# A two-layer hybrid trunk on one core: all engines in written order, evictions one block of weights apart, v from blocks of 256 rows, rotations between the conv blocks

## The chip, the core and the metric

The kernel runs on one core of a Trainium2 chip. The time is device microseconds; the median of 3 runs of the kernel before is 892.13 us (891.50 to 892.79). Five engines work side by side, each through its own list of instructions: TensorE (PE; its weight loads are shown as PEld), VectorE (DVE), ScalarE (ACT), GpSimd (POOL) and SyncE (SP, which here only starts DMAs). TensorE's granted clock is 1.2 or 2.4 GHz; the profile writes it as a share of full speed.

## The reference

```python
def hybrid_layer(x, ...):
    h = rmsnorm(x, norm_mix)
    cb, cc, cu, q, k, v, g, ga, gb = split(h @ w_in)
    y_conv = (cb * causal_conv3(cc * cu)) @ w_conv_out
    o = retention(rotary(q), rotary(k), v)           # 4 heads, decayed causal scores
    o = (o - mean(o)) * rsqrt(var(o) + EPS) * ret_norm
    y_ret = (silu(g) * o) @ w_ret_out
    x = x + (sigmoid(ga) * y_conv + sigmoid(gb) * y_ret) @ w_o
    h2 = rmsnorm(x, norm_mlp)
    return x + square(relu(h2 @ w_up)) @ w_down
# two layers, then a final rmsnorm; 256 tokens, width 1024, d_ff 4096, float32
```

## The kernel before

All weights are cut on the host into 152 blocks of 1 MB (128 partitions x 2048 float32), 76 a layer: 32 of w_in (1024 contraction rows x 256 columns each), 4 each of w_conv_out (`yc`), w_ret_out (`yr`) and w_o (`mg`), 16 of w_up and 16 of w_down. They pass in one fixed order, and every block goes through the same stations. SP starts its DMA into a `raw` buffer. ACT rounds it to a high part (`split`, L99), in two halves of 128 x 1024, and DVE subtracts (L100) to get the low part; both stand in a `parts` buffer. PE then does 16 pairs of products (`proj`, L171 and L172): high weights against high and low activations (512 columns), low weights against high activations (256 columns). The result, in a PSUM tile `ps`, is evicted by `collect` (L209 on ACT, L210 on DVE), and what follows (rotation, gate, conv) is done on DVE, ACT and POOL.

There are 3 `raw` buffers, 3 `parts` buffers and 3 `ps` tiles. Blocks are split up to AHEAD = 2 ahead (`next_block`). Small work that belongs to later blocks is put off by a number of blocks (`later`). The program is recorded in this order, but `schedule_with_timeline_sim=True` lets a scheduler, by its own simulated times, choose the order in which each engine's instructions stand.

The w_in blocks of a layer come as v (4), four triples cc, cu, cb of the conv branch, q (2), k (2), g (4), ga (4), gb (4). In layer 0 the first v block is multiplied in plain float32 without being split (`whole_tokens`, L130 to L140), while its data arrives in five pieces, each with a piece of `px` (x and the gains), all on SP. Six products on zeros (`warm`, L319) come ahead. A v block gives one head of v for all tokens; `value` (L407 to L416) reduces it on DVE (L409), subtracts the mean on POOL (L412), and splits it. The sums over all channels that a norm needs are two small products with ones (`mix_st`, `mlp_st`, and `var_ps` for the heads; L231 and L232).

Of the kernel before, what the change touches and what calls it, by code (L numbers as in the profile page):

```python
# [28 lines left out]
FIRST = ((1, 1, 2, 2, 2), (2, 2, 4), (4, 4))  # L29
AHEAD = 2  # L30
WARM = 6


Q0, K0, V0, G0, GA0, GB0 = 3072, 3584, 4096, 5120, 6144, 7168
IN_ORDER = (
    [("v", V0 + 256 * i) for i in range(4)]
    + [(n, o + 256 * i) for i in range(4) for n, o in (("cc", 1024), ("cu", 2048), ("cb", 0))]
    + [("q", Q0), ("q", Q0 + 256), ("k", K0), ("k", K0 + 256)]
    + [("g", G0 + 256 * i) for i in range(4)]
# [3 lines left out]
BLOCKS_PER_LAYER = 32 + 4 * 3 + 16 + 16  # L43
# [5 lines left out]
def trunk_kernel(ctx, tc, px, pos, w, cst, mask, out):  # L49
# [4 lines left out]
    raw_p = ctx.enter_context(tc.tile_pool(name="raw", bufs=3))  # L54
# [17 lines left out]
    idle = tmp.tile([P, 2 * T], BF16, tag="tmp", bufs=5, name="idle")  # L72
# [8 lines left out]
    class Parts:  # L81


        def __init__(self, name):
            self.tiles = [s8.tile([P, KT // 2, 2, T], F32R, tag="s8", name=f"{name}{i}") for i in range(2)]
# [9 lines left out]
    def t2(name, tag="tmp", bufs=5):  # L95
        return tmp.tile([P, 2, T], F32, tag=tag, bufs=bufs, name=name)
# [14 lines left out]
    def load_block(i):  # L111
        raw, parts = block_tiles()
        nc.sync.dma_start(out=raw.rearrange("p a b -> p (a b)"), in_=w[i])
        for p in range(2):
            split_block(raw, parts, slice(p * KT, (p + 1) * KT))
        return parts

    cnt = [0]

    ready = {}  # L120

    def next_block():
        i = cnt[0]
        cnt[0] += 1
        for j in range(i, min(i + AHEAD + 1, w.shape[0])):
            if j not in ready:
                ready[j] = load_block(j)
        return ready.pop(i)

    def whole_tokens(xs):  # L130

        ps = ps_main.tile([P, 2, 2, T], F32, tag="mm", name="ps")
        raw = next_block()
        for k in range(KT):
            for j in range(2):
                mm(ps[:, j, 0], xs[:, k, j * P:(j + 1) * P], raw[:, 2 * k:2 * k + 2, :], k == 0, k == KT - 1)
        run_waiting()
        t = t2("sum", "sum", 4)
        nc.scalar.copy(t, ps[:, :, 0, :])
        return t  # L140


    waiting = []

    def later(n, fn, *args):
        waiting.append([cnt[0] + n, fn, args])

    def run_waiting(everything=False):
        while True:
            due = [e for e in waiting if everything or e[0] <= cnt[0]]  # L150
            if not due:
                return
            waiting.remove(due[0])
            due[0][1](*due[0][2])
# [4 lines left out]
    def proj(act, n_blocks=1):  # L159

        ps = ps_main.tile([P, 2, 2, T], F32, tag="mm", name="ps")
        for b in range(n_blocks):
            blk = next_block()
# [6 lines left out]
            run_waiting()  # L173
        return ps

    def proj_one(act, plus, n_blocks=2):
# [3 lines left out]
        for b in range(n_blocks):  # L180
            blk = next_block()
# [5 lines left out]
            if b == 0:  # L187
                for part in range(2):
                    mm(ps, ident, plus[:, part], False, False)
            run_waiting()  # L190
        return ps

    def proj_tokens(act):

        ps = ps_main.tile([P, 2, 2, T], F32, tag="mm", name="ps")
        blk = next_block()
        for k in range(KT):
            a = act.at(k)
            for j in range(2):
                c = slice(j * P, (j + 1) * P)  # L200
                mm(ps[:, j], a[:, 0, c], blk[:, :, 2 * k:2 * k + 2, :], k == 0, False)
                mm(ps[:, j, 1], a[:, 1, c], blk[:, 0, 2 * k:2 * k + 2, :], False, k == KT - 1)
        run_waiting()
        return ps
# [14 lines left out]
    def rsqrt(y, v, scale, alloc):  # L219

        m, a = alloc("rs_m"), alloc("rs_a")
# [4 lines left out]
        for _ in range(3):  # L226
            newton(y, a, m)

    def column_sums(o, hi, lo):

        tc.keep_in_program_order(nc.tensor.matmul(o, lhsT=ones, rhs=hi, start=True, stop=False))  # L231
        nc.tensor.matmul(o, lhsT=ones, rhs=lo, start=False, stop=True)  # L232

    class Norm:
# [8 lines left out]
        def split(self, k):  # L243
            g = self.gain[:, k:k + 1]
            a = self.act.at(k)
            nc.scalar.activation(a[:, 0], x[:, k, :], AF.Copy, scale=g)
# [4 lines left out]
        def square(self, p, in_order=False):  # L251
            xs = x[:, 2 * p:2 * p + 2, :]
            sq = self.sum if p == 0 else t2("sq")
            ins = nc.scalar.activation(sq, xs, AF.Square)  # L254
            if in_order:
                tc.keep_in_program_order(ins)
            if p:
                nc.gpsimd.tensor_tensor(out=self.sum, in0=self.sum, in1=sq, op=ALU.add)  # L258

        def pair(self, p):  # L260
            for k in (2 * p, 2 * p + 1):
                self.split(k)
            self.square(p)

        def fold(self):
            a, b = self.sum[:, 0, :], self.sum[:, 1, :]
            nc.gpsimd.tensor_tensor(out=a, in0=a, in1=b, op=ALU.add)
            self.sums = tuple(tmp.tile([P, T], F32R, tag="tmp", bufs=5, name=f"{self.name}_{n}") for n in ("sh", "sl"))
            split(a, *self.sums)

        def total(self):

            st = ps_misc.tile([P, T], F32, tag="misc", name=f"{self.name}_st")
            column_sums(st, *self.sums)
            return st
# [10 lines left out]
    nc.vector.memset(eps, EPS)  # L286

    nc.scalar.activation(eps2, eps, AF.Square)
    norm = Norm(gains(0, G_MIX), "mix0")
    w3 = [w[i].rearrange("p (a b) -> p a b", b=P) for i in range(len(FIRST))]  # L290
    begun = [(raw_p.tile([P, 2 * KT, P], F32, tag="raw", name="raw"), None)] + [block_tiles() for _ in FIRST[1:]]
    k0 = 0
    for n in FIRST[0]:
        c = slice(n_par + k0 * T if k0 else 0, n_par + (k0 + n) * T)
        nc.sync.dma_start(out=px_sb[:, c], in_=px[:, c])
        nc.sync.dma_start(out=begun[0][0][:, 2 * k0:2 * (k0 + n), :], in_=w3[0][:, 2 * k0:2 * (k0 + n), :])
        k0 += n
    for i in range(1, len(FIRST)):
        k0 = 0
        for n in FIRST[i]:  # L300
            nc.sync.dma_start(out=begun[i][0][:, 2 * k0:2 * (k0 + n), :], in_=w3[i][:, 2 * k0:2 * (k0 + n), :])
            k0 += n

    xs = stile("xs")
    for k in range(KT):
        nc.vector.tensor_scalar(
            out=xs[:, k, :], in0=x[:, k, :], scalar1=norm.gain[:, k:k + 1], scalar2=None, op0=ALU.mult
        )
        if k % 2:
            split(xs[:, k - 1:k + 1, :], *norm.act.pair(k // 2))  # L310
    for k in range(0, KT, 2):
        split_block(*begun[1], slice(2 * k, 2 * k + 4))
    for k in range(0, KT, 4):
        split_block(*begun[2], slice(2 * k, 2 * k + 8))
    ready.update([(0, begun[0][0])] + [(i, begun[i][1]) for i in range(1, len(FIRST))])

# [436 lines left out]
```

## Time and profile before

| | us |
|---|---|
| median of 3 runs | 892.13 |
| profiled execution | 892.27 |
| its span | 890.1 |
| PE busy | 877.3 (99%) |
| DVE busy | 695.9 (78%) |
| ACT busy | 505.4 (57%) |
| POOL busy | 251.7 (28%) |
| mean granted clock | 0.994 |

The span is what the engines and DMAs work in; 2.2 us of the execution lie around it. PE's share says that little time is idle there, but not that it always runs at its best pace: the duration of one block does. DVE's 78% is a mean: it is nearly full in the w_in blocks of a layer and half empty in the MLP.

### The profile page before, as it was taken

Reading aid. Unit: us, or ns where it says so; the run is one execution under the profiler, and the core shown is the slowest. Engines: PE = TensorE matmul, PEld = TensorE weight load, DVE = VectorE, ACT = ScalarE, POOL = GpSimd, SP = SyncE. Lnnn points to the kernel's source line nnn. Section 1 sums busy time; section 2 is a strip of 40 time slices with the busy share of each in tenths; the row PEclk is TensorE's granted clock in tenths of the full one; section 3 lists DMA queues with packets and bytes.
Section 4 is the critical chain, followed back from the end, with each engine's and each line's share of the span. In section 5 each row is a group of like instructions: output and inputs, shape, how many; then the busy total and the mean of one; then the engine's idle time right before and its main releaser. Section 6 shows DMA issues by size and latency. Waiting matters only on the chain.

```text
span 890.1 us, 12685 instructions
## 1 busy us (share of the span) xinstructions
PE 877.3 (99%) x5090; PEld 767.9 (86%) x5090; DVE 695.9 (78%) x785; ACT 505.4 (57%) x700; POOL 251.7 (28%) x170
## 2 busy tenths in 40 slices
PE   8999999999999999999999999999999999999996
PEld 6878888888888888888888888888888888888896
DVE  5989999799977966555588989998996897664451
ACT  6445636675556877444455554566654597764440
POOL 2883353421003322000046324443200323210110
PEclk9999999999999999999999999999999999999998
DMA  9645645444654655555545553555355555555521
GB/s 319 233 141 190 205 159 199 179 159 148 231 188 143 237 193 188 192 192 188 193 179 190 189 190 142 189 190 177 130 215 189 189 180 206 189 200 190 191 75 48
DMA packets 24682, 163.00 MB, mean 183 GB/s; under 512 B 2864, under 2 KB 3504, under 8 KB 5552
## 3 DMA queue, kind: packets, MB, share of 16 engines
q1 hardware_dynamic: 24336, 161.68, 51.3%
q8 instruction: 40, 0.66, 0.3%
q10 hardware_dynamic: 288, 0.52, 0.2%
q14 instruction: 18, 0.15, 0.0%
HBM read 161.14 MB, written 1.05 MB: 182 GB/s over the span
## 4 chain that ended last, share of the span: by engine, by line
PE 92%; POOL 3%; DVE 2%; DMA 1%; ACT 1%; issue 0%; SPq 0%; DVEq 0%; POOLq 0%; ACTq 0%
PE ps L157 89%; PE o_ps L157 1%; DVE parts L100 1%; POOL sum L412 1%; DMA raw<-w 1%; PE sc_ps L157 1%; DMA px_sb<-px 0%; ACT parts L99 0%; POOL v L412 0%; POOL mix_sum L258 0%; POOL red L333 0%; POOL sum L432 0%; DVE o L675 0%; POOL turns L339 0%; DVE rs_a L215 0%
## 5 line engine op out<-in xcount | busy, mean ns | idle before, releaser
L100 DVE TENSOR_TENSOR parts<-raw,parts 128x1024 fp32r<-128x1024 f32 (+1 forms) x304 | 411.2, 1384 | 70.4 <-ACT parts L99 69.5
L99 ACT CAST parts<-raw 128x1024 fp32r<-128x1024 f32 (+1 forms) x304 | 302.4, 1044 | 109.2 <-PE ps L157 78.1
L157 PE MATMUL ps<-mix,parts 128*128 128x512 f32 (+1 forms) x1792 | 323.0, 341 | 2.5 <-DVE parts L100 2.5
L157 PEld LDWEIGHTS ps<-mix,parts 128*128 128x128 f32 x1792 | 275.9, 189 | 44.0 <-DVE parts L100 2.8
L157 PE MATMUL ps<-up,parts 128*128 128x512 f32 (+1 forms) x1088 | 179.4, 326 | 0.0
L157 PE MATMUL ps<-mlp,parts 128*128 128x256 f32 (+1 forms) x1024 | 178.5, 335 | 0.0
L157 PEld LDWEIGHTS ps<-up,parts 128*128 128x128 f32 x1088 | 159.1, 188 | 19.6
L157 PEld LDWEIGHTS ps<-mlp,parts 128*128 128x128 f32 x1024 | 155.4, 188 | 22.4 <-issue 0.4
L210 DVE TENSOR_TENSOR sum<-ps,sum 128x512 f32<-128x512 f32 x87 | 59.4, 683 | 43.7 <-ACT sum L209 43.7
L209 ACT COPY sum<-ps 128x512 f32<-128x512 f32 x87 | 50.6, 582 | 75.2 <-PE ps L157 75.2
L594 POOL TENSOR_TENSOR u<-u,rr2m 128x512 f32<-128x512 f32 x32 | 47.7, 1492 | 123.4 <-ACT u L604 106.1
L258 POOL TENSOR_TENSOR mix_sum<-mix_sum,sq 128x512 f32<-128x512 f32 x8 | 12.6, 1574 | 145.1 <-ACT sq L254 145.1
L258 POOL TENSOR_TENSOR mlp_sum<-mlp_sum,sq 128x512 f32<-128x512 f32 x6 | 12.9, 2158 | 122.7 <-ACT sq L254 122.7
L157 PE MATMUL ps<-yr,parts 128*128 128x512 f32 (+1 forms) x256 | 44.7, 336 | 0.0
L157 PE MATMUL ps<-mg,parts 128*128 128x512 f32 (+1 forms) x256 | 44.7, 336 | 0.0
L157 PE MATMUL ps<-yc,parts 128*128 128x512 f32 (+1 forms) x256 | 44.7, 336 | 0.0
L157 PEld LDWEIGHTS ps<-yc,parts 128*128 128x128 f32 x256 | 39.1, 188 | 5.2
L157 PEld LDWEIGHTS ps<-yr,parts 128*128 128x128 f32 x256 | 39.1, 188 | 5.2
L157 PEld LDWEIGHTS ps<-mg,parts 128*128 128x128 f32 x256 | 39.1, 188 | 5.2
L157 PE MATMUL ps<-parts,mix 128*128 128x512 f32 (+1 forms) x224 | 39.8, 338 | 0.0
L157 PEld LDWEIGHTS ps<-parts,mix 128*128 128x128 f32 x224 | 34.2, 188 | 5.0
L100 DVE TENSOR_TENSOR up<-u,up 128x512 fp32r<-128x512 f32 x32 | 26.1, 820 | 0.0
(175 smaller groups left out, 666.6 us busy)
## 6 DMA issues: line engine op xcount, KB each, us to landing
raw<-w SPq DMA_DIRECT2D x149, 1024.0 KB, 4.8
raw<-w SPq DMA_DIRECT2D x3, 512.0 KB, 7.5
raw<-w SPq DMA_DIRECT2D x5, 256.0 KB, 6.1
px_sb<-px SPq DMA_DIRECT2D x3, 256.0 KB, 4.6
mask_sb<-mask SPq DMA_DIRECT2D x1, 512.0 KB, 7.2
out<-o SPq DMA_DIRECT2D x2, 256.0 KB, 2.3
out<-o ACTq DMA_DIRECT2D x2, 256.0 KB, 2.5
raw<-w SPq DMA_DIRECT2D x2, 128.0 KB, 2.7
```

Source lines behind the costliest of these rows:

```text
L99: nc.scalar.copy(hi, src)
L100: nc.vector.tensor_tensor(out=lo, in0=src, in1=hi.bitcast(F32), op=ALU.subtract)
L157: nc.tensor.matmul(o, lhsT=a, rhs=b, start=start, stop=stop, skip_group_check=True)
L209: nc.scalar.copy(t, ps[:, :, 1, :])
L210: nc.vector.tensor_tensor(out=t, in0=ps[:, :, 0, :], in1=t, op=ALU.add)
L258: nc.gpsimd.tensor_tensor(out=self.sum, in0=self.sum, in1=sq, op=ALU.add)
L412: nc.gpsimd.tensor_scalar(out=o_, in0=t[:, c, :], scalar1=mu[:, c:c + 1], scalar2=None, op0=ALU.subtract)
L594: nc.gpsimd.tensor_tensor(out=u, in0=u, in1=both(rr2), op=ALU.mult)
```

## The change

The scheduler is taken away (`tc.manual_schedule()`), and all instructions stand as they are written. The function `window(products)` writes what belongs to one block i of weights: evictions and other work that earlier windows put there with `at(n, fn, ..., ph)`; the high and low parts of both halves of block i+2 (from i = 3 on; the parts of the first blocks, 0 to 5, are placed by `first_parts`); the products of block i; the DMA of block i+3; and small products (`products_at`). So the eviction of block i-1 is written into window i, and what depends on it into window i+1. There are 2 `raw` buffers.

```diff
+    def window(products):
         i = cnt[0]
+        todo = work.setdefault(i, [])
...
+        run(-1)
+        run(0)
+        if i > 2:
+            split_half(i + 2, 0)
+        run(1)
+        if i > 2:
+            split_half(i + 2, 1)
+        run(2)
+        products(blocks[i])
+        if i == 0:
+            load_block(2)
+        load_block(i + 3)
...
+    def first_parts(norm=norm):
...
+        at(0, parts, 1, 2, 3)
+        at(1, parts, 2, 4, 5)
+        at(2, parts, 3, 6, 7)
+        at(3, norm.split, 0)
+        for i, half in ((4, 0), (4, 1)):
+            at(3, split_half, i, half)
...
+        for half in range(2):
+            at(3, split_half, 5, half, ph=2)
```

The v blocks now hold 256 contraction rows x 1024 columns each. All four add into two PSUM tiles, each of two heads, with 24 products of 512 columns per block; only contraction tile 0 of layer 0 is multiplied in plain float32 (4 products). `value` reads PSUM itself:

```diff
+        for n in range(4):
+            window(lambda blk: products(blk, n))
...
+        def value(i, ps):
...
+            nc.vector.tensor_reduce(out=mu, in_=vs, axis=mybir.AxisListType.X, op=ALU.add)
+            nc.vector.tensor_scalar(out=mu, in0=mu, scalar1=-1.0 / T, ...)
+            for n in range(2):
...
+                nc.scalar.activation(hi, vs[:, 0, n, :], AF.Identity, bias=mu[:, 0, n:n + 1])
+                nc.vector.scalar_tensor_tensor(out=lo, in0=vs[:, 0, n, :], ..., in1=hi.bitcast(F32), ...)
+                nc.scalar.activation(v1[:, h, :], vs[:, 1, n, :], AF.Identity, bias=mu[:, 1, n:n + 1])
```

`px` comes in three pieces on ACT's queue, block 0 in three pieces and block 1 whole on SP's; there are 10 warm products. The order of the w_in blocks changes, and the blocks after v are:

```diff
+    [("g", G0), ("g", G0 + 256)]
+    + _conv(0) + _conv(1)
     + [("q", Q0), ("q", Q0 + 256), ("k", K0), ("k", K0 + 256)]
+    + _conv(2) + _conv(3)
+    + [("g", G0 + 512), ("g", G0 + 768)]
```

The norm factor, the rotation tables, scores, mixed values, head roots and head outputs are each cut into steps one window apart; the head gain is folded into the gating product; the sum of the two branches moves to POOL (except the last); w_o's and w_down's evictions into x are done per 256 columns.

On DVE, at the end of layer 0's v blocks (in these names `parts_N` holds the split weights of one block, `raw_N` its DMA target, `ps_N` a PSUM tile), there stands after the change:

```order
L276 SCALAR_TENSOR_TENSOR mix00_103<-px_sb_90,mix00_103 128x256
L104 TENSOR_TENSOR parts_214<-raw_213,parts_214 128x1024 x2
L104 TENSOR_TENSOR parts_249<-raw_248,parts_249 128x1024 x4
L462 TENSOR_REDUCE mu_320<-ps_146 128x4
L463 TENSOR_SCALAR mu_320<-mu_320 128x4
L468 SCALAR_TENSOR_TENSOR v0_parts_142<-ps_146,mu_320,v0_parts_142 128x256 x2
L104 TENSOR_TENSOR parts_297<-raw_296,parts_297 128x1024 x2
L104 TENSOR_TENSOR mix0_sl_370<-mix0_sum_102,mix0_sh_369 128x256
L462 TENSOR_REDUCE mu_373<-ps_147 128x4
L463 TENSOR_SCALAR mu_373<-mu_373 128x4
L468 SCALAR_TENSOR_TENSOR v0_parts_142<-ps_147,mu_373,v0_parts_142 128x256 x2
```

Before, in the same place:

```order
L100 TENSOR_TENSOR parts_106<-raw_105,parts_106 128x512 x4
L409 TENSOR_REDUCE mu_206<-sum_204 128x2
L100 TENSOR_TENSOR parts_108<-raw_107,parts_108 128x1024
L410 TENSOR_SCALAR mu_206<-mu_206 128x2
L100 TENSOR_TENSOR parts_108<-raw_107,parts_108 128x1024
L100 TENSOR_TENSOR v0_parts_169<-sum_204,v0_parts_169 128x256
L210 TENSOR_TENSOR sum_258<-ps_213,sum_258 128x512
L409 TENSOR_REDUCE mu_261<-sum_258 128x2
L410 TENSOR_SCALAR mu_261<-mu_261 128x2
L100 TENSOR_TENSOR parts_215<-raw_214,parts_215 128x1024 x2
L100 TENSOR_TENSOR v0_parts_169<-sum_258,v0_parts_169 128x256
```

The reduction of v (L462, before L409) stood between the halves of the next blocks, each after one v block; now the first stands behind six lo halves, of blocks 4 and 5 (those of 5 twice), and the second behind those of block 6.

On DVE, at the entry to the q blocks (`acc` is the conv's sum, `yc` its split output, `rot` a rotated half), there stands after the change:

```order
L236 TENSOR_TENSOR sum<-ps,sum 128x512
L104 TENSOR_TENSOR parts<-raw,parts 128x1024 x2
L518 TENSOR_TENSOR sum<-sum,acc 128x512
L104 TENSOR_TENSOR yc_426<-sum,yc_426 128x2x256
L236 TENSOR_TENSOR sum<-ps,sum 128x512
L449 TENSOR_TENSOR rot<-sum,sinq 64x512
L450 TENSOR_TENSOR rot<-sum,sinq 64x512
L104 TENSOR_TENSOR parts<-raw,parts 128x1024 x2
L104 TENSOR_TENSOR q_parts<-qk,q_parts 128x512
L236 TENSOR_TENSOR sum<-ps,sum 128x512
```

Before:

```order
L210 TENSOR_TENSOR sum<-ps,sum 128x512
L100 TENSOR_TENSOR parts<-raw,parts 128x1024
L449 TENSOR_TENSOR sum<-sum,acc 128x512
L100 TENSOR_TENSOR parts<-raw,parts 128x1024
L100 TENSOR_TENSOR yc_172<-sum,yc_172 128x2x256
L210 TENSOR_TENSOR sum<-ps,sum 128x512
L398 TENSOR_TENSOR rot<-sum,sinq 64x512
L399 TENSOR_TENSOR rot<-sum,sinq 64x512
L100 TENSOR_TENSOR parts<-raw,parts 128x1024 x2
L100 TENSOR_TENSOR q_parts<-qk,q_parts 128x512
```

The rotation windows hold the same instructions in the same order; what changed is that they come after the second conv triple of the layer, in the order's 13th to 16th block, where before they came after the fourth.

## Rows read from the trace of the kernel before

**Rows 1.** The page's part 1: engine, busy us, share of the span, instructions

```profile
PE 877.3 (99%) x5090; PEld 767.9 (86%) x5090; DVE 695.9 (78%) x785; ACT 505.4 (57%) x700; POOL 251.7 (28%) x170
```

**Rows 2.** Waits of TensorE (PE): line waited for, us in total, times, longest

```profile
PE ps L157 <- DVE parts L100: 2.5, 1, 2.5
PE ps L157 <- DMA raw<-w: 1.2, 2, 0.9
```

**Rows 3.** Timeline of PE, first 31 us: start, us, operation, [idle before <-releaser]

```profile
1.17 2.74 PE L319 MATMUL warm<-idle 128*128 128x512 bf16 x6 [1.17 <-DVE eps L286]
3.79 2.88 PE L157 MATMUL ps<-raw,xs 128*128 128x256 f32 x8
...
9.88 3.69 PE L157 MATMUL ps<-raw,xs 128*128 128x256 f32 x16 [0.32 <-DMA raw<-w]
13.22 17.00 PE L157 MATMUL ps<-parts,mix 128*128 128x512 f32 x96
30.06 1.08 PE L157 MATMUL ps<-mix,parts 128*128 128x512 f32 x5
```

**Rows 4.** Timeline of PE around 67 us

```profile
67.04 5.34 PE L157 MATMUL ps<-mix,parts 128*128 128x256 f32 x20 [2.46 <-DVE parts L100]
```

**Rows 5.** Windows: us, busy PE PEld DVE ACT POOL, PEclk, DMA, GB/s

```profile
67.09:70.50 3.41, 3.41 (x11) 2.92 (x12) 2.73 (x4) 1.75 (x3) 0.00 (x0) 0.50 0.38 108
...
109.00:137.00 28.00, 28.00 (x163) 24.39 (x162) 27.68 (x25) 11.57 (x16) 16.20 (x8) 1.00 0.44 151
```

**Rows 6.** Timeline of PE, pace of the blocks in both layers

```profile
200.50 22.35 PE L157 MATMUL ps<-yc,parts 128*128 128x512 f32 x128
222.69 22.35 PE L157 MATMUL ps<-yr,parts 128*128 128x512 f32 x128
...
456.12 0.28 PE L231 MATMUL mix_st<-mix_sh,ones 128*128 128x256 f32 x1
...
467.65 96.26 PE L157 MATMUL ps<-mix,parts 128*128 128x512 f32 x544
563.75 0.53 PE L157 MATMUL sc_ps<-q_parts,k_parts 128*128 128x256 f32 x3
```

**Rows 7.** Timeline of DVE, 30 to 136 us

```profile
30.95 0.68 DVE L210 TENSOR_TENSOR sum<-ps,sum 128x512 f32<-128x512 f32 x1
...
69.40 0.69 DVE L100 TENSOR_TENSOR yc<-sum,yc 128x512 fp32r<-128x512 f32 x1 [0.69 <-ACT yc L99]
...
78.92 1.21 DVE L100 TENSOR_TENSOR parts<-raw,parts 128x1024 fp32r<-128x1024 f32 x1
...
81.25 3.45 DVE L100 TENSOR_TENSOR parts<-raw,parts 128x1024 fp32r<-128x1024 f32 x2
...
95.63 3.45 DVE L100 TENSOR_TENSOR parts<-raw,parts 128x1024 fp32r<-128x1024 f32 x2
...
109.41 0.68 DVE L210 TENSOR_TENSOR sum<-ps,sum 128x512 f32<-128x512 f32 x1
...
130.47 0.68 DVE L210 TENSOR_TENSOR sum<-ps,sum 128x512 f32<-128x512 f32 x1
```

**Rows 8.** Timeline of POOL, around 81 us

```profile
81.41 2.21 POOL L545 TENSOR_TENSOR sum<-sum,rr 128x512 f32<-128x512 f32 x1 [4.10 <-DVE sum L210]
```

**Rows 9.** The page's part 6: issues, KB each, us from issue to landing

```profile
raw<-w SPq DMA_DIRECT2D x149, 1024.0 KB, 4.8
```

**Rows 10.** Lines of ACT, 30 to 200 us: busy, mean ns | idle before

```profile
L99 ACT CAST parts<-raw 128x1024 fp32r<-128x1024 f32 x58 | 58.0, 1049 | 2.0 <-PE ps L157 2.0
...
L99 ACT CAST v_parts<-sum 128x256 fp32r<-128x256 f32 x2 | 0.8, 407 | 7.7 <-POOL sum L412 7.7
```

**Rows 11.** Lines of DVE, 30 to 200 us, the same columns

```profile
L100 DVE TENSOR_TENSOR parts<-raw,parts 128x1024 fp32r<-128x1024 f32 x57 | 90.2, 1609 | 1.6 <-ACT parts L99 1.3
...
L409 DVE TENSOR_REDUCE mu<-sum 128x2 f32<-128x512 f32 x2 | 1.3, 673 | 0.0
...
L410 DVE TENSOR_SCALAR mu<-mu 128x2 f32<-128x2 f32 x2 | 0.5, 260 | 0.0
```

More of the change, by code (lines that the diff above doesn't have):

```diff
@@ L148, in run_waiting, with at, products_at @@
[L148 to L154, printed above, removed]
+    cnt = [0]
+    work, small_products = {}, {}
+    raws, blocks = {}, {}
+    def at(n, fn, *args, ph=0):
+        work.setdefault(cnt[0] + n, []).append((ph, fn, args))
+    def products_at(n, fn, *args):
+        small_products.setdefault(cnt[0] + n, []).append((fn, args))
@@ L164, in proj, with products @@
         ps = ps_main.tile([P, 2, 2, T], F32, tag="mm", name="ps")
-        for b in range(n_blocks):
-            blk = next_block()
+        def products(blk, b):
             for k in range(KT):
@@ L172, in proj @@
                     mm(ps[:, j, 1], blk[:, 1, 2 * k + j, :], a[:, 0], False, end)
-            run_waiting()
+        for b in range(n_blocks):
+            window(lambda blk: products(blk, b))
         return ps
@@ L179, in proj_one, with products @@
         n = 2 * KT
-        for b in range(n_blocks):
-            blk = next_block()
+        def products(blk, b):
             for k in range(n):
@@ L286, in trunk_kernel @@
     nc.vector.memset(eps, EPS)
-    nc.scalar.activation(eps2, eps, AF.Square)
[L289 to L315, printed above, removed]
+    norm = Norm(gains(0, G_MIX), "mix0")
+    for i in range(2):
+        raws[i], blocks[i] = block_tiles()
+    w0 = w[0].rearrange("p (a b) -> p a b", b=P)
+    k0 = 0
+    for n in (1, 3, 4):
+        c = slice(n_par + k0 * T if k0 else 0, n_par + (k0 + n) * T)
+        nc.scalar.dma_start(out=px_sb[:, c], in_=px[:, c])
+        k0 += n
+    for c in (slice(0, 4), slice(4, 8), slice(8, 16)):
+        nc.sync.dma_start(out=raws[0][:, c, :], in_=w0[:, c, :])
+    nc.sync.dma_start(out=raws[1].rearrange("p a b -> p (a b)"), in_=w[1])
+    nc.scalar.activation(eps2, eps, AF.Square)
+    xs = tmp.tile([P, T], F32, tag="tmp1", bufs=6, name="xs")
+    nc.vector.tensor_scalar(out=xs, in0=x[:, 0, :], scalar1=norm.gain[:, 0:1], scalar2=None, op0=ALU.mult)
+    norm.split(1)
+    split_half(0, 1)
     warm = ps_misc.tile([P, 2 * T], F32, tag="misc", name="warm")
@@ new lines, in add_to_x @@
+        def add_to_x(p, ps, scale, norm, parts=True):
+            for j in range(2):
+                xk = x[:, 2 * p + j, :]
+                for half in (1, 0):
+                    nc.vector.scalar_tensor_tensor(
+                        out=xk, in0=ps[:, j, half, :], scalar=scale, in1=xk, op0=ALU.mult, op1=ALU.add
+                    )
+            if parts:
+                for j in range(2):
+                    norm.split_hi(2 * p + j)
+                for j in range(2):
+                    norm.split_lo(2 * p + j)
+            at(0, norm.square, p, ph=1)
+            if p == NPAIR - 1:
+                at(0, norm.fold, ph=1)
+                at(1, norm.split_sum)
```

495 lines of the change are left out of this document (270 added, 225 removed).

## The prediction

> **What bounds the kernel now.** I read four views, from the coarse to the fine. The page's part 1 first: PE is busy 877.3 of 890.1 us, so only 12.8 us lie between the kernel and a PE that never waits, and at most those are to be had from waits [rows 1]. The list of PE's waits next: beside the head and the tail there is one wait, 2.5 us for DVE's low parts, and two short ones for weights, 1.2 us together [rows 2]. The timeline then places them: the short ones in the first block, the long one at 67.04 us, in the middle of a conv block [rows 3, 4]. The windows show what comes after it: the granted clock is 0.50, its lower level of 1.2 GHz, from 67.09 to 70.50 us, just after PE had been idle for 2.46 us, and half of that time, 1.7 us, is lost as well [rows 4, 5]. So the stall costs 4.2 us in all.
>
> A last look goes to the pace. From 200.50 to 222.69 us PE does four blocks in 22.19 us, 5.55 each; from 467.65 to 563.75 us it does 17 blocks (544 of 32 products), 5.65 each [rows 6]. No wait is shown there. The slow pace begins in layer 1 at the norm's column sum at 456.12 us and ends with the head sums; 27 blocks at 0.106 us make 2.9 us a layer. I don't know what sets it.
>
> DVE is the second resource. A rotation block takes it (130.47 - 109.41) / 3 = 7.02 us (two more evictions lie between), against PE's 5.65, and from 109 to 137 us it is busy 27.68 of 28 [rows 5, 7]. A conv triple takes DVE 95.63 - 81.25 = 14.38 us against PE's 3 x 5.65 = 16.95 [rows 7]. So the four rotation blocks put DVE behind by 4 x (7.02 - 5.65) = 5.5 us, and each conv triple gives 2.6 back. Before, four triples come ahead of the rotations; now two.
>
> **The change part by part.** The sum starts from the profiled execution, 892.27 us, 0.14 over the median of the runs.
>
> *Head.* The first block's 16 plain products (32 records, 0.23 each at the end [rows 3]) take 7.4 us at that rate. Its new form is 4 of 512 columns, so the same 16 records, 3.7 us, and 20 further products of 512 columns; by the pace of a block (16 x 768 columns in 5.55 us) one of those takes 0.231, together 4.6. The sum is 8.3 us, 0.9 more, but it needs no more data, and can hide the 1.25 us of waits behind an x that comes on another queue. Block 4 began at 30.06 us. I take 0.6 off, between -1.3 (all waits gone) and +1.3 (as much again). The other three v blocks have 24 x 512 = 12,288 columns as before, so they cost the same: 0.
>
> *The stall at 67 us goes: -4.2.* It came where DVE, from 30.95 to 69.40 us, had twelve halves and what the scheduler put between them [rows 7]. Its place is in the new order another block with other work. What is late next are the two following items.
>
> *The first eviction of v, new.* Block 5's products use the PSUM tile of the first two heads again, and block 6's that of the other two, and the third tile goes to block 4: this is what now stands behind the v blocks. Let L be the landing of block 1. Two halves of high parts and low parts are one cast and two subtractions, with an x split of 0.4 between them: 1.05 + 2 x 1.21 + 0.4, about 3.8 [rows 7, 10]. With two raw buffers block 3's DMA waits for that, 4.8 us to land [rows 9], 3.8 to split, block 5's again 4.8: L + 17.2. Block 5's halves stand twice in DVE's list ahead of the reduction, 1.05 + 4 x 1.21 = 5.9: L + 23.1. Then the reduction of 1024 elements (2 x 0.67), its scale (0.26) and ACT's four passes over PSUM (0.41 each) [rows 10, 11], 3.2: L + 26.3. PE starts block 1 after its first cast, at L + 1.05, and wants block 5 after four blocks of 5.5, at L + 23.1. So PE waits 3.2 us. For block 6 the second eviction follows two more halves, 2.4 + 0.4 + 1.6 on DVE and 1.6 on ACT: 6.0 after the first against the 5.55 of block 5, about 0.5 to 1.5 more; I take 1.0. Together +4.2. It is 0 if the data are earlier by that much (block 3 sooner by its own slack), and 5.9 with half clock behind the wait as at 67 us.
>
> *DVE's lag at the q and k blocks.* In the first conv blocks DVE did six blocks' work in 69.40 - 30.95 = 38.5 us; seven windows (4 to 10, with the norm factor and the gates in them) are then 45 us. They begin with the v eviction, at about 34.4, and end at 79.8; the two last conv windows take 4.8 each, to 89.4. PE, with block 4 at 29.5 and 4.2 of waits, begins block 13 at 29.5 + 4.2 + 9 x 5.6 = 84.1, so DVE is 5.3 behind there. It may be late by two blocks less its own work of 6.3 us up to the second low half: 11.1 - 6.3 = 4.8. The lag at the fourth rotation is 5.3 + 3 x 1.4 = 9.5, and 9.5 - 4.8 = 4.7 us would be waited. The stretch that I scaled includes DVE's own waits, 3 us of them for other engines, so it can be nothing: 0 to 4.7, and I take the middle, +2.4. In layer 1 the lag starts from nothing and reaches 3 x 1.4 = 4.2, under 4.8: 0.
>
> The low part of a half takes DVE 1.21 us at 78.92, but of the two that start at 81.25 the first lies under POOL's 2.21 us at 81.41, and the two take 3.45, 1.0 more than 2 x 1.21 [rows 7, 8]. So each wide POOL operation that falls on a DVE operation costs DVE about 1 us; the 1.61 mean of 57 halves holds that [rows 11]. The Trainium skill's page "SBUF — State Buffer", section "Who interferes with whom", says that a DVE operation with two SBUF inputs and a GpSimd operation that reads SBUF exclude each other, and that issue order decides who waits. The trace agrees, with 3.45 for two. By the rule a written order that puts rotations, conv and POOL's new additions in one window gives no overlap back: one more such meeting in each of seven windows would make the 45 us into 52.
>
> *Pace.* Waits at block halves and column sums are placed anew. That the slow stretches remain, end or grow is open; I count one of the two layers at 5.55: -2.9, between -5.8 and +2.9 (as many blocks more).
>
> *Everything else at nothing.* The finer steps of scores, values, roots and head outputs run on DVE and ACT while PE does ga, gb and `yc`; their cover is a DVE at 78% on the mean; without it a window is 1 to 2 us too long. The sum of the branches on POOL is covered the same way. The tail is unchanged. Dropping the third raw buffer costs nothing while 4.8 us per DMA stay under a block's 5.55; its price appears only in the v term.
>
> Sum: 892.27 - 0.6 - 4.2 + 4.2 + 2.4 - 2.9 = 891.2 us.
>
> **The rivals.** *Faster, 885 us.* DVE is not late: v's eviction costs 0.5 (data earlier), the q blocks 0, and one layer gets the better pace: -0.6 - 4.2 + 0.5 - 2.9 = -7.2. For it: DVE's waits in the stretch, and the halves that are always two blocks ahead. Against it: the duplicate halves of block 5 and DVE at 27.68 of 28 in rotations.
>
> *Slower, 898 us.* In written order DVE never makes up its lag: evictions stand ahead of the halves, so PE waits at rotations for low parts. It costs the full 4.2 + 4.7, two drops of the clock at 1.7, and no better pace: -0.6 - 4.2 + 8.9 + 3.4 = +7.5 with both drops, +5.8 with one; 898 with one. It decides once DVE is over 4.8 us behind at block 13. For it: two conv triples recover only half of what four did. Against it: the scheduler's own order stalled PE only once.
>
> *No change of the pace, 894 us.* All as forecast but for the pace, which stays in both layers: 891.2 + 2.9 = 894.1. Nothing in the rows decides against it.
>
> **How the numbers follow.** A measurement tells 0.2%, 1.8 us, from no change: faster is under 890.3, slower over 893.9. The forecast has 0.34, its own range 888.5 to 893.9, of which 0.13 faster, 0.19 same, 0.02 slower; the pace rival 0.16 (0.04 same, 0.12 slower); the faster rival 0.28; the slower one 0.22. That makes faster 0.41, same 0.23, slower 0.36. The range takes in most of both sides: 884 to 899.
>
> **What would show it.** PE's waits after the change: none at 67 us; one of 2 to 5 us on ACT's v writes at the start of block 5, about 35 us, with a clock of 0.50 behind it if the term is larger; waits on DVE's parts in layer 0's q and k blocks (2.4 us, or none, or over 4.7); blocks of layer 1 at 5.55 or 5.65. A PE busy below 875 us would prove the pace; a wait in conv, gate or MLP blocks, on POOL or on a DMA, would make the prediction wrong, and so would a head longer by over 1.3 us.

## The result, and the profile after

The change makes the kernel slower: 945.75 us (median of 4 runs, 945.40 to 947.85) against 892.00, a ratio of 1.0607 (95% interval 1.0588 to 1.0625). The forecast was 891.2 us, with a range from 884 to 899.

The page's part 1 (engine, busy us, share of the span) and PE's waits (line waited for, us in total, times, longest) of the kernel after, to set beside [rows 1, 2]:

```profile
PE 898.1 (95%) x5026; PEld 772.1 (82%) x5026; DVE 709.9 (75%) x800; ACT 510.5 (54%) x709; POOL 230.0 (24%) x160
```

```profile
PE ps L165 <- DVE parts L104: 18.4, 37, 1.7
PE ps L165 <- ACT v L472: 7.0, 3, 4.6
PE var_ps L165 <- DVE osq L104: 6.1, 2, 3.1
PE ps L165 <- DVE mlp L276: 3.1, 2, 1.9
```

The span grew from 890.1 to 943.6 us, and no engine has much more to do: DVE is busy 14 us longer, POOL 22 us less, and all shares fall. The 53.5 us are not work; they are time in which each engine waits for another. PE's one wait for low parts has become 37, none longer than 1.7 us. Of PE's 21 us more of busy time about 10 are the lower clock: it stands at 0.50 in six stretches, 23.9 us together, ahead of the tail, where there was one of 3.41, and half of each is lost.

Where it went, by the starts of the blocks in PE's timeline (blocks in the order in which they pass, both layers added, us):

| stage | before | after |
|---|---|---|
| start of block 0 | 3.8 | 5.5 |
| v | 49.0 | 46.0 |
| first four blocks behind v | 45.4 | 56.0 |
| the next eight | 94.7 | 95.4 |
| the next four (after: rotations evicted) | 45.2 | 52.1 |
| the last four before ga | 49.7 | 52.7 |
| ga | 54.5 | 50.8 |
| gb | 46.8 | 55.6 |
| w_conv_out | 44.4 | 53.3 |
| w_ret_out, w_o | 88.7 | 90.0 |
| w_up | 178.3 | 193.6 |
| w_down and the tail | 189.6 | 192.7 |

Small products stand in other blocks after: three of a layer's four scores (0.58 us each) moved into "the next four", and two of its four weighted values (1.17 each) out of ga. So 3.5 of the 6.9 us more in "the next four" are moved work, and so is ga's gain.

The largest item, 15.3 us, is in w_up, where the prediction expected nothing. The views below are DVE, ACT and PE in one of its windows, after (start, us, operation, idle before and its releaser):

```profile
341.05 2.63 DVE L104 TENSOR_TENSOR parts<-raw,parts 128x1024 fp32r<-128x1024 f32 x2 [2.31 <-ACT parts L103]
343.61 0.68 DVE L104 TENSOR_TENSOR up<-u,up 128x512 fp32r<-128x512 f32 x1
344.21 0.68 DVE L236 TENSOR_TENSOR sum<-ps,sum 128x512 f32<-128x512 f32 x1
347.19 1.48 DVE L104 TENSOR_TENSOR parts<-raw,parts 128x1024 fp32r<-128x1024 f32 x1 [2.30 <-ACT parts L103]
```

```profile
342.39 0.58 ACT L235 COPY sum<-ps 128x512 f32<-128x512 f32 x1
344.92 0.63 ACT L710 ACTIVATE sum<-sum 128x512 f32<-128x512 f32 x1 [1.95 <-DVE sum L236]
345.59 0.63 ACT L711 ACTIVATE u<-sum 128x512 f32<-128x512 f32 x1
346.13 1.99 ACT L103 CAST parts<-raw 128x1024 fp32r<-128x1024 f32 x2
```

```profile
342.60 5.83 PE L165 MATMUL ps<-mlp,parts 128*128 128x256 f32 x32 [0.32 <-DVE parts L104]
348.73 5.83 PE L165 MATMUL ps<-mlp,parts 128*128 128x256 f32 x32 [0.30 <-DVE parts L104]
```

Read it as a ring. DVE subtracts two halves (341.05), then a low part of `up`, then adds the eviction (344.21 to 344.89). ACT's relu waits for that sum, its square follows, and only then, behind them in its written order, the cast of the next half (346.13 to 347.16); DVE's next subtraction waits for the cast (347.19). Once around takes 347.19 - 341.05 = 6.14 us, of which DVE idles 2.30 and ACT 1.95. PE's blocks start 348.73 - 342.60 = 6.13 us apart, and not 5.55. Neither engine is full; the two halves are still meant for two blocks later, but a lead doesn't help when every turn of the ring takes longer than a block: it is eaten, and then the ring is the pace. Before, ACT's list had the casts and the split of `up` ahead of relu (L603):

```profile
306.96 2.00 ACT L99 CAST parts<-raw 128x1024 fp32r<-128x1024 f32 x2
308.86 0.61 ACT L99 CAST up<-u 128x512 fp32r<-128x512 f32 x1
309.38 0.63 ACT L603 ACTIVATE sum<-sum 128x512 f32<-128x512 f32 x1
```

The rotations look alike, but there DVE is full. DVE, ACT and POOL after, then a window (columns as in [rows 5]):

```profile
121.00 0.68 DVE L236 TENSOR_TENSOR sum<-ps,sum 128x512 f32<-128x512 f32 x1
121.71 0.69 DVE L449 TENSOR_TENSOR rot<-sum,sink 64x512 f32<-64x512 f32 x1
122.41 1.69 DVE L450 TENSOR_TENSOR rot<-sum,sink 64x512 f32<-64x512 f32 x1
124.14 3.46 DVE L104 TENSOR_TENSOR parts<-raw,parts 128x1024 fp32r<-128x1024 f32 x2
127.52 0.41 DVE L104 TENSOR_TENSOR k_parts<-qk,k_parts 128x256 fp32r<-128x256 f32 x1
127.85 0.68 DVE L236 TENSOR_TENSOR sum<-ps,sum 128x512 f32<-128x512 f32 x1
```

```profile
119.69 0.41 ACT L103 CAST k_parts<-qk 128x256 fp32r<-128x256 f32 x1 [4.11 <-POOL qk L451]
120.00 0.58 ACT L235 COPY sum<-ps 128x512 f32<-128x512 f32 x1
120.48 2.00 ACT L103 CAST parts<-raw 128x1024 fp32r<-128x1024 f32 x2
```

```profile
121.76 1.80 POOL L447 TENSOR_TENSOR qk<-sum,cosk 128x512 f32<-128x512 f32 x1 [2.10 <-DVE sum L236]
124.25 2.26 POOL L451 TENSOR_TENSOR qk<-qk,rot 128x512 f32<-128x512 f32 x1 [0.69 <-DVE rot L450]
```

```profile
109.93:131.34 21.41, 18.55 (x109) 15.74 (x107) 21.22 (x19) 8.58 (x12) 12.57 (x6) 1.00 0.43 153
```

A turn takes 127.85 - 121.00 = 6.85 us. ACT idles 4.11 us for POOL ahead of the split of k, with the copy of the next eviction behind it, so that a path returns here too. But DVE is busy 21.22 of 21.41 us, two of its operations in each turn lengthened beside POOL's (1.69 against 0.69 us, 3.46 against the 2 x 1.21 that the prediction read from [rows 7]). DVE's own work, POOL's meetings with it included, is enough to set this pace, and ACT's idle time costs nothing.

In gb the loss is one wait in each layer, of PE for the second head sum, whose input is the low part of `osq`. PE, then DVE, after:

```profile
198.31 0.51 PE L165 MATMUL var_ps<-osq,ones 128*128 128x512 f32 x1 [3.08 <-DVE osq L104]
```

```profile
187.87 3.34 DVE L577 RECIPROCAL rm<-rm 128x512 f32<-128x512 f32 x1
197.84 0.42 DVE L104 TENSOR_TENSOR osq<-osq 128x256 fp32r<-128x256 f32 x1
```

DVE is busy 10.32 of the 10.39 us from 187.87 to 198.26, so this product is due before a full DVE reaches its input; it is no ring. Behind each of the two waits (3.08 and 3.04 us) the clock stands at 0.50 for 3.41 us. w_conv_out is mixed: in layer 0 DVE is busy 6.23 of the first block's 6.30 us, and 4.77 of the second's 6.02.

Another place is v. PE after, then the window of the lower clock behind it (columns as in [rows 5]), then DVE and ACT ahead of it:

```profile
29.35 5.80 PE L165 MATMUL ps<-mix,parts 128*128 128x512 f32 x32
39.73 8.65 PE L165 MATMUL ps<-mix,parts 128*128 128x512 f32 x32 [4.58 <-ACT v L472]
```

```profile
39.09:45.92 6.83, 6.19 (x19) 5.33 (x20) 4.97 (x6) 2.97 (x5) 6.32 (x7) 0.50 0.23 70
```

```profile
30.19 5.16 DVE L104 TENSOR_TENSOR parts<-raw,parts 128x1024 fp32r<-128x1024 f32 x4 [1.92 <-ACT parts L103]
35.27 1.22 DVE L462 TENSOR_REDUCE mu<-ps 128x4 f32<-128x1024 f32 x1
```

```profile
36.79 0.47 ACT L467 ACTIVATE v_parts<-ps,mu 128x256 fp32r<-128x256 f32 x1 [2.16 <-DVE mu L463]
37.81 0.47 ACT L472 ACTIVATE v<-ps,mu 128x256 f32<-128x256 f32 x1 [0.55 <-DVE v_parts L468]
38.18 0.47 ACT L467 ACTIVATE v_parts<-ps,mu 128x256 fp32r<-128x256 f32 x1
39.20 0.47 ACT L472 ACTIVATE v<-ps,mu 128x256 f32<-128x256 f32 x1 [0.55 <-DVE v_parts L468]
```

Block 5 waits from 35.15 to 39.73 us for the last of these passes; behind the wait the clock stands at 0.50 for 6.83 us, where it was 3.41 after the stall before [rows 4, 5].

### The profile page after: what moved, and what is told of

It is laid out like the page before. It is cut to its first block, busy times and chain, and to the rows that moved or that the text cites. A ratio compares the mean times of both kernels' runs of the same rounds, so it can differ in the third digit from the quotient of the medians.

```text
span 943.6 us, 12548 instructions
## 1 busy us (share of the span) xinstructions
PE 898.1 (95%) x5026; PEld 772.1 (82%) x5026; DVE 709.9 (75%) x800; ACT 510.5 (54%) x709; POOL 230.0 (24%) x160
## 4 chain that ended last, share of the span: by engine, by line
DVE 44%; PE 25%; ACT 18%; issue 8%; POOL 3%; DMA 3%; SPq 0%; DVEq 0%; ACTq 0%; POOLq 0%
DVE parts L104 26%; PE ps L165 24%; ACT parts L103 8%; DVE sum L236 4%; DMA raw<-w 3%; ACT sum L710 2%; ACT u L711 2%; DVE up L104 2%; DVE rot L450 1%; DVE px_sb L683 1%; POOL ta L490 1%; ACT sum L235 1%; DVE acc L504 1%; ACT L572 1%; DVE sum L518 1%
## 5 line engine op out<-in xcount | busy, mean ns | idle before, releaser
L104 DVE TENSOR_TENSOR parts<-raw,parts 128x1024 fp32r<-128x1024 f32 x305 | 436.2, 1465 | 155.4 <-ACT parts L103 154.1
L103 ACT CAST parts<-raw 128x1024 fp32r<-128x1024 f32 x305 | 306.2, 1047 | 89.4 <-DMA raw<-w 60.2
L165 PE MATMUL ps<-mix,parts 128*128 128x512 f32 (+1 forms) x1792 | 329.0, 345 | 15.0 <-DVE parts L104 7.4
L165 PE MATMUL ps<-mlp,parts 128*128 128x512 f32 (+1 forms) x1024 | 185.9, 341 | 7.9 <-DVE parts L104 4.8
L712 POOL TENSOR_TENSOR u<-u,rr2m 128x512 f32<-128x512 f32 x32 | 41.8, 1308 | 153.3 <-ACT u L711 136.2
L236 DVE TENSOR_TENSOR sum<-ps,sum 128x512 f32<-128x512 f32 x78 | 53.1, 680 | 2.4 <-ACT sum L235 1.8
L710 ACT ACTIVATE sum<-sum 128x512 f32<-128x512 f32 x32 | 20.2, 632 | 63.5 <-DVE sum L236 63.5
L235 ACT COPY sum<-ps 128x512 f32<-128x512 f32 x78 | 45.1, 578 | 6.8 <-PE ps L165 6.8
L165 PE MATMUL ps<-mg,parts 128*128 128x512 f32 (+1 forms) x256 | 45.4, 338 | 0.1
L165 PE MATMUL ps<-parts,mix 128*128 128x512 f32 x180 | 41.5, 390 | 1.0 <-ACT parts L103 1.0
L631 POOL TENSOR_TENSOR sum<-sum,rr 128x512 f32<-128x512 f32 x8 | 12.2, 1527 | 76.7 <-DVE sum L236 76.7
```

The lines of the kernel that those rows point to most:

```text
L103: nc.scalar.copy(hi, src)
L104: nc.vector.tensor_tensor(out=lo, in0=src, in1=hi.bitcast(F32), op=ALU.subtract)
L165: nc.tensor.matmul(o, lhsT=a, rhs=b, start=start, stop=stop, skip_group_check=True)
L235: nc.scalar.copy(t, ps[:, :, 1, :])
L236: nc.vector.tensor_tensor(out=t, in0=ps[:, :, 0, :], in1=t, op=ALU.add)
L631: nc.gpsimd.tensor_tensor(out=z, in0=z, in1=both(rr2), op=ALU.mult)
```

## The experiments

Two theories stood at first: that the written order makes ACT, DVE and POOL wait for each other in turn (the rings), and that something else in the change does (the order of blocks, v, two raw buffers, DVE's load).

**Casts first.** `split_half` in two, the casts at the window's head:

```diff
+        if i > 2: cast_half(i + 2, 0); cast_half(i + 2, 1)
         run(-1)
         run(0)
-        if i > 2: split_half(i + 2, 0)
+        if i > 2: sub_half(i + 2, 0)
```

> All of the change, but in every window ACT's two casts of block i+2 stand ahead of the evictions; DVE's order is as after. Theory 1 (a ring through ACT and DVE in written order: low halves, add, relu, square, cast, low half, 6.13 us around in the w_up blocks, and its like in the gate and head windows): the ring is cut, w_up blocks go from 6.13 to 5.55, and the time from 945.8 to about 915 to 925; the waits on ACT's v writes at block 5 stay. Rival (two raw buffers: the casts wait for weights): the casts still wait for the same DMAs, blocks stay at 6.13, about 945.

Measured 979.78 us, a miss in the total. Blocks 48 to 59 (w_up) do go from 71.0 to 66.56 us, 5.55 each, so the ring there is cut. But two casts, 2.0 us, now stand ahead of every eviction, also of those that PE waits for at once. Its waits in this run:

```profile
PE ps L180 <- DVE parts L145: 22.4, 24, 1.7
PE ps L180 <- DVE mg L104: 13.3, 4, 4.6
```

**Relu and square late**, in w_up windows alone:

```diff
-            nc.scalar.activation(rl, rl, AF.Relu)
-            nc.scalar.activation(u, rl, AF.Square)
+            at(0, relu_square, ph=2)
```

> All of the change, but relu and square of a w_up block stand behind the casts of its window, in w_up windows alone. Theory 1 (the ring): w_up blocks 5.55 in place of 6.13, some 24 blocks in the two layers with 0.58 each, so 945.8 - 14 = about 932, nothing else moves. Rival (raw buffers or the POOL port): w_up blocks stay over 6, within 2 us of 945.8.

Measured 930.50 us: 15.2 less, of which w_up gives 12.2 and w_down 3.2 (the lag that spilled into it). ACT and PE of this run:

```profile
330.42 0.59 ACT L235 COPY sum<-ps 128x512 f32<-128x512 f32 x1 [1.36 <-PE ps L165]
330.91 2.00 ACT L103 CAST parts<-raw 128x1024 fp32r<-128x1024 f32 x2
332.81 0.63 ACT L713 ACTIVATE sum<-sum 128x512 f32<-128x512 f32 x1
```

```profile
302.49 77.81 PE L165 MATMUL ps<-mlp,parts 128*128 128x512 f32 x448
```

ACT now idles for PE, as it should, and PE does 14 blocks without a break. Nothing was taken away, only two instructions moved behind two others; neither the two raw buffers nor POOL sets the pace here. The ring is shown for w_up.

**The scheduler back**, all else of the change kept:

```diff
-    with tile.TileContext(nc) as tc, tc.manual_schedule():
+    with tile.TileContext(nc, schedule_with_timeline_sim=True) as tc:
```

> All of the change except the written order: the scheduler orders the engines as it did before. If the written order is the cause (theory 1), most of the 54 us goes: 890 to 905. If the new order of blocks, the v blocks or two raw buffers are the cause (theory 2), it stays over 930.

Measured 901.68 us (899.48 and 903.89): the written order is worth some 44 of the 54 us, whatever the paths by which it costs them. gb, yc, w_ret_out and w_o return to their old times; 13.7 us more than before are left in the first four blocks behind v.

**The kernel before in its written order**, its scheduler and its two pins of single instructions taken out, nothing else:

```diff
-    with tile.TileContext(nc, schedule_with_timeline_sim=True) as tc:
+    with tile.TileContext(nc) as tc, tc.manual_schedule():
```

> The kernel before, with its instructions in the order in which it records them (no scheduler), nothing else changed: three raw buffers, old v, old block order. Theory 1 (written order makes engines wait for each other in turn): over 920, and with work not cut into steps a window apart perhaps far over 950, w_up blocks over 5.55. Theory 2 (order of blocks, v, raw buffers): 890 to 900.

Measured 1031.28 us. So written order costs that program 139 us, and the changed one 44. That the cutting into steps, a window apart, makes the difference is likely and not shown, as the two programs differ in other things too.

**Block 5 split once**:

```diff
-        for half in range(2):
-            at(3, split_half, 5, half, ph=2)
```

> All of the change, but block 5 of layer 0 is split once, not twice. If the duplicate stands in the way of v's first eviction, as forecast: the eviction starts 2.3 us sooner (two low halves), PE's wait of 4.6 us at block 5 becomes about 2.3, and of the 3.4 us that the lower clock takes behind it none or half stays: 945.8 goes to 940 to 943.5. Rival (the wait is set by the weights' landing, or by DVE's other work): within 1 us of 945.8.

Measured 945.30 us, a miss. Block 5 starts 1.0 us sooner, not 2.3, and the clock behind it is low for 3.41 us only; block 12 starts 1.8 us sooner; but blocks 12 to 15 take 26.3 us in place of 24.0, so that the gain is given back there.

**The order of blocks alone**, put into the kernel before, under its scheduler (scores begin at the third `cc`, as in the change, and the rotation tables two blocks sooner):

```diff
+    + [("g", G0), ("g", G0 + 256)]
+    + [(n, o + 256 * i) for i in range(2) for n, o in (("cc", 1024), ("cu", 2048), ("cb", 0))]
     + [("q", Q0), ("q", Q0 + 256), ("k", K0), ("k", K0 + 256)]
+    + [(n, o + 256 * i) for i in range(2, 4) for n, o in (("cc", 1024), ("cu", 2048), ("cb", 0))]
+    + [("g", G0 + 512), ("g", G0 + 768)]
```

> The kernel before, with the new order of the w_in blocks alone (gates 0 and 1, two conv triples, q and k, two conv triples, gates 2 and 3), under the scheduler, old v blocks. If the order of blocks costs by itself (two triples recover only half of what four do): q and k blocks wait 3 to 5 us in each layer, 896 to 902. If it is harmless: the stall at 67 us moves or goes, 886 to 894.

Measured 894.63 us (8 runs, ratio 1.0029, 1.0017 to 1.0040), between the two expectations. Blocks 16 to 19 of layer 0 take 31.6 us in place of 22.6, of which 2.3 are the four scores that stand in them now; the rest is a wait for k of 3.1 us at the first of them and the low clock behind it, 6.83 us from 108.6. In layer 1 they take 24.9, which is the scores and nothing else. The stall at 67 us is gone (-3.1 in blocks 8 to 11). So the lag of DVE at the early rotations is real in layer 0, some 6.7 us, and about half of it is paid by the stall.

**Late steps**: besides relu and square, the splits of rotated q and k, tanh of all gates, conv sums and outputs, weighted scores, the split of `osq` and head outputs go behind the casts of their window, and the head sums one block later, such as

```diff
-            at(1, lambda: nc.scalar.activation(d, d, AF.Tanh, scale=0.5))
+            at(1, lambda: nc.scalar.activation(d, d, AF.Tanh, scale=0.5), ph=2)
```

> The change with relu and square late (as in the run before), and also the other steps that wait for POOL or DVE put behind the casts of their window: splits of rotated q and k, tanh of all gates, conv sums and outputs, weighted scores, head outputs; head sums one block later. Theory 1 (each of these stands at the head of ACT's window and holds the casts, so that windows go around in 6.1 to 6.9 us): rotation blocks from 6.85 to about 5.65 to 6, gb and yc blocks to 5.55, 930.5 goes to 908 to 915. Rival (DVE has too much work there, or the POOL lock sets the pace): under 5 us gained, 925 or more.

Measured 926.31 us, a miss, and on the rival's side. Against the run with relu and square late gb falls from 55.5 to 45.7 us, now without the wait for the head sum, which comes a block later; w_conv_out falls from 53.2 to 46.5, by which of the edits isn't told apart. But the rotation blocks rise from 51.5 to 61.7. PE there, and the window of the rotations:

```profile
127.00 0.39 PE L165 MATMUL sc_ps<-q_parts,k_parts 128*128 128x256 f32 x1 [3.69 <-DVE k_parts L104]
```

```profile
109.93:131.34 21.41, 17.41 (x81) 15.01 (x82) 21.25 (x20) 7.36 (x11) 11.69 (x6) 0.84 0.42 147
```

With the path through ACT cut, a turn of the rotation still takes DVE 7.12 us (112.92 to 120.04), and it is still full (21.25 of 21.41): the rival's DVE, and no ring, is the limit there. The late split of k is too late for the first scores, and w_ret_out and w_o lose 4 us in the same way (waits on `mg`).

**Late steps and block 5 split once**, the two edits above together:

> The run before this (late steps) with block 5 split once as well. Both effects should add: 2 to 6 us less than with the late steps alone, 903 to 912. If that shows no more than 1 us, PE's wait at block 5 is set elsewhere.

Measured 926.42 us (923.91 and 928.92), a miss: nothing gained, as alone.

**v copied out of PSUM at once**, two copies of 128 x 1024 on ACT, means and splits from SBUF later:

```diff
+        def value_copy(i, ps):
+            vc = kept["vc"][:, 4 * i:4 * i + 4, :]
+            nc.scalar.copy(vc, ps.rearrange("p j (h f) -> p (j h) f", f=T))
+            at(2 - i, value, i, vc, ph=2)
```

> All of the change (written order, block 5 split twice), but the two PSUM tiles of v are emptied by one copy each on ACT at the head of the window after the last v block, and means and splits are taken from SBUF later. If the long eviction of v (reduce, then six steps in turn on ACT and DVE, 4.4 us) holds the PSUM tiles that blocks 5 and 6 want: block 5 waits at most 1 us in place of 4.6, no lower clock behind it, and layer 1 loses its 3.0 us at blocks 80 to 83: 945.8 goes to 934 to 939. Rival (the weights' own parts are as late, which splitting block 5 once hints at): under 3 us gained.

Measured 945.37 us, a miss in the total. The wait is gone where it was: blocks 4 to 7 take 23.6 us in place of 30.4, layer 1's 22.6 in place of 25.6. It returns at block 9, where PE waits 4.37 us for a cast, with the low clock, and blocks 8 to 11 take 32.3 in place of 26.2.

**Late steps with the scores two blocks later**:

```diff
-                    products_at(1 + h, scores, h)
+                    products_at(3 + h, scores, h)
```

> Late steps (ring cut everywhere) with the scores two blocks later than there. The late splits of k made PE wait for k at the first scores (3.7 and 3.4 us, with the lower clock behind). If that alone ate the gain of the late steps: 926.3 goes to 914 to 919. If not: 923 or more.

Measured 935.49 us, a miss. The wait for k goes (blocks 16 to 19 from 34.0 to 28.8 us), and one for the weighted scores comes, in both layers:

```profile
160.66 0.98 PE L165 MATMUL o_ps<-sc_parts,v_parts 128*128 128x256 f32 x3 [5.12 <-DVE sc L535]
```

**Late steps without those of q and k**, against the late steps:

```diff
-                at(1, split, d, q_parts[:, 0, h, :], q_parts[:, 1, h, :], ph=2)
+                at(1, split, d, q_parts[:, 0, h, :], q_parts[:, 1, h, :])
```

> Late steps, but the splits of rotated q and k at the head of the window as the change has them. With the late splits, PE waited for k at the first scores. If that alone ate the gain there: blocks 16 to 19 of layer 0 go from 34.0 back to 26 to 28 us, those of layer 1 from 27.7 to 25.5, so 926.3 goes to 914 to 919. If other waits take their place: 922 or more.

Measured 918.96 us, the best in written order: 7.4 less than with them. Blocks 16 to 19 go from 34.0 to 29.8 us in layer 0 and from 27.7 to 24.9 in layer 1, less than expected in the first and more in the second.

**All cuts together**, in written order: the late steps and late scores, v copied, block 5 split once, and the branch sum and x splits of the output projections behind the casts:

```diff
-            nc.gpsimd.tensor_tensor(out=m, in0=ta[:, s, :], in1=b, op=ALU.add)
-            at(1, split, m, *mg.pair(p))
+            nc.vector.tensor_tensor(out=m, in0=ta[:, s, :], in1=b, op=ALU.add)
+            at(0, split, m, *mg.pair(p), ph=2)
```

> Written order with every ring found so far cut: late steps, late scores, v copied out of PSUM at once, block 5 split once, the sum of the branches back on DVE with its split in the same window behind the casts, x splits and squares of the first three w_o blocks behind the casts. Theory 1 (rings and the long v eviction are all of it): 892 to 903. Rival (written order costs by itself, as no order fixed beforehand fits the POOL and DVE meetings): 905 or more.

Measured 924.83 us, a miss, and the rival's side. ACT of this run:

```profile
45.44 2.00 ACT L103 CAST parts<-raw 128x1024 fp32r<-128x1024 f32 x2
54.18 0.51 ACT L470 ACTIVATE v_parts<-vc,mu 128x256 fp32r<-128x256 f32 x1 [6.75 <-DVE mu L466]
```

ACT stands 6.75 us before one instruction whose mean DVE hasn't reached, with the eviction and two casts of another block behind it. But this run doesn't decide between theory and rival: it has the late scores in it, which alone had cost 9.2 us, and the same wait for weighted scores (5.14 and 5.08 us), so that its blocks 20 to 23 take 69.2 us where the scheduled program takes 51.0. The other cuts with q and k split early, as in the run before, were not tried together. That an order without such places exists isn't excluded; none of the nine written orders tried is one.

**The scheduler, v copied out, block 5 split once**, and (later) **the scheduler with block 5 split once alone**, made of the edits above:

> The changed program under the scheduler, with v copied out of PSUM at once and block 5 split once. Under the scheduler alone (901.7) one wait of 8.5 us at blocks 5 to 7 stood for nearly all of what was left over before. If that is the v tiles: 889 to 895, the best of the changed program so far. If it is DVE's load there: 898 or more.

> The changed program under the scheduler with block 5 split once, v's PSUM tiles emptied as the change does it. From 901.7 (split twice, no copy) to 888.3 (split once, copy) two things had changed. If the long eviction is the cause: 899 to 903 here, with the wait on the gate's eviction near block 6 still 6 us or more. If the duplicate was: 888 to 891.

Measured 888.28 us (4 runs; ratio 0.9962, 0.9942 to 0.9982), 0.4% less than before, and 896.75 us (894.87 to 898.53), between the second run's two expectations. So under the scheduler the long eviction is worth 8.5 us. The duplicate's 4.9 are not clear of the noise (901.68 came from runs at 899.48 and 903.89), and in the profiles blocks 4 to 7, where it stands, give only 2.3. The rows below name the first gate's eviction, which DVE reaches with the scheduler alone at 44.70 us, among its passes over v; with v copied it comes at 42.52, and PE doesn't wait for it. PE at block 5, with the scheduler alone, with block 5 split once, and with v copied too:

```profile
45.43 14.90 PE L165 MATMUL ps<-mix,parts 128*128 128x512 f32 x69 [8.53 <-DVE sg L236]
```

```profile
43.49 16.78 PE L165 MATMUL ps<-mix,parts 128*128 128x512 f32 x84 [6.98 <-DVE sg L236]
```

```profile
31.65 78.59 PE L165 MATMUL ps<-mix,parts 128*128 128x512 f32 x444
```

**The squares of layer 0 kept in program order** on top of that:

```diff
-            nc.scalar.activation(sq, xs, AF.Square)
+            ins = nc.scalar.activation(sq, xs, AF.Square)
+            if self.name == "mix0":
+                tc.keep_in_program_order(ins)
```

> The scheduler with v copied out (888.3), and layer 0's four squares kept in program order on ACT as the kernel before does it: there they stood ahead of the casts of blocks 1 and 2, and PE waited 0.9 + 0.5 + 0.5 us for parts in the v blocks. If those casts are late because of the squares: the waits go, block 4 starts at 29.5 to 30.5 in place of 31.65, 886 to 887.5. If the weights' landing sets them: 888 to 889.

Measured 890.74 us (10 runs, ratio 0.9996, 0.9983 to 1.0009), a miss. Block 4 does start at 30.71 in place of 31.65, but so it does without the edit in the run with block 5 split once alone, and waits of 0.88 and 0.94 us for parts are left in the v blocks. The work put off comes due at the rotations: blocks 12 to 19 take 51.2 us in place of 46.9, with waits of 1.1 to 1.3 us for low parts.

## Why the prediction was wrong

The parts of the sum, against the profiled execution:

*Head, -0.6.* The number is right, block 4 at 29.35 us where 29.46 was forecast and 30.06 measured before; the parts are not, and they cancel. PE starts block 0 at 5.47 and not 3.79 us. The block's plain products take 3.70 us as forecast (in 8 records, not 16), but 12 further products follow and not 20, since contraction tile 0 stands for 12 of a block's 24. The three other v blocks, put at 0, take 5.44 us each, 0.5 less together.

*The stall at 67 us, -4.2.* It goes from its place, but blocks 10 to 12 wait for low parts again and, with a stretch of the lower clock, take 22.1 us where three blocks without a wait take 17.0 and the three with the stall took 21.2. Nothing was gained.

*v's first eviction, +4.2.* The right place and mechanism, under-sized. The wait was put at 3.2 and is 4.58 us, on ACT's v writes as forecast, since ACT and DVE take the passes over v in turn (36.79 to 39.67 us, 2.9 where 1.6 was counted): ACT idles 0.55 us for DVE ahead of each second pass, which reads the tile's other half. Why it waits there isn't shown; over a copy in SBUF (all cuts together) the four ACT passes follow each other without a gap, 43.36 to 44.57. The low clock behind the wait, which was left to the bounds, takes 3.4 us more. The second eviction, put at 1.0, shows no wait in layer 0; layer 1, put at nothing, loses 3.0. Of the duplicate halves, which the chain counted in full, a removal in written order gave back 1.0 us there and nothing in the end.

*DVE's lag at q and k, +2.4 and 0.* Right, and nearly so in size. Blocks 16 to 19 take 27.5 us in layer 0 and 24.6 in layer 1; four blocks at 5.65 with the three scores that stand in them now take 24.3. That leaves 3.2 and 0.3. (In the forecast's working 34.4 + 45 is 79.4, not 79.8, which changes little.) The 7.0 us of DVE for a rotation, which came from the rows, is there (6.85 a turn), with DVE full. The order of blocks alone, under the scheduler, shows a lag in layer 0 and none in layer 1 too.

*Pace, -2.9.* Not had: blocks 84 to 91 stay at 5.65. Even the sign hangs on something else (below).

*Everything else at nothing.* This is the step that failed. It took "a DVE at 78% on the mean" as cover for the finer steps and gave no price to the order in which they stand. In w_up DVE has 3.8 us of work a window and ACT 4.2 (23.07 and 25.00 us in the six from 348.04 to 384.93); both fit in 5.55, and the window takes 6.13. What sets it is the path that goes through both in the order written, back to its own start. Under the scheduler ACT's casts stood ahead of the steps that wait (306.96 to 309.38 above); taking it away was costed at nothing. The term should have held w_up (+15.3), w_down and tail (+3.1), gb (+8.8) and w_conv_out (+8.9), some 36 of the 54 us: in w_up and behind it for the ring, in gb for a small product due before its input. The prediction's own sign of being wrong, a wait in conv, gate or MLP blocks, is what came. The slower rival named the right edit (written order), and its mechanism, a DVE with too much to do, holds at the rotations; but its price was 6 us, and it had nothing for the MLP.

What the runs settle: written order some 44 us (945.75 to 901.68) and the long eviction of v 8.5 under the scheduler (896.75 to 888.28); the duplicate's part is not clear of the noise. With the scheduler back, block 5 split once and v copied, the rest of the change (order of blocks, v blocks, finer steps, the head) is worth 3.4 us in the other direction (888.28 against 891.64 before, in the same comparison). In written order each of v's two edits gave nothing. The ring is shown by a cut for w_up alone; gb's wait is read from the trace and went with the edit that moved its product; the causes within w_conv_out are not told apart; at the rotations DVE is full.

## What to carry to other kernels

In an order fixed by hand, count for every window not only each engine's work but the longest path that returns to its own start through two or three engines, written order included; it must be under the window's time, whatever the lead. Put first on each engine what other engines need soonest (copies out of PSUM), then what waits for nothing (casts of the next weights; ahead of the copies they cost 34 us here), and steps that wait for another engine behind it, but not behind their own user's due time. Look first whether an engine on the path is full: where it is, as DVE at the rotations, moving the others' steps doesn't shorten the turn. Emptying a PSUM tile by one copy, where the next block wants it, was worth 8.5 us under the scheduler, and in written order it only moved the wait.

## What the runs showed of the hardware that was not expected

The two paces of PE, 5.55 and 5.65 us a block, belong to no stage. The same blocks of the same products run at either: with the scheduler and block 5 split once PE does 319 products in 55.40 us, 5.56 a block, where the run with v copied takes 78.59 us for 444, 5.66. Rows of PE, the first of them:

```profile
54.80 55.40 PE L165 MATMUL ps<-mix,parts 128*128 128x256 f32 x319
```

In layer 1 blocks 84 to 91 take 45.2 us after, and 44.4 with relu and square late, though nothing in those blocks was edited. The pace changes at waits and column sums and then lasts for up to tens of blocks; what decides it stays open, and it moves such comparisons by 1 to 3 us. Second, how long the lower clock lasted didn't follow the length of the wait ahead of it. It was 6.83 us behind the wait of 4.58 and 3.41 behind that of 2.46 before [rows 4, 5]; but also 6.83 behind one of 3.06 (the order of blocks alone), 3.41 behind one of 3.62 (block 5 split once) and 3.41 behind one of 1.34 (after, at 78.92 us).
